# Gates matrix of a product-key expert layer made once for all 128 first parts, a quarter kept in SBUF and the rest read back from DRAM in blocks

## The chip, the cores and the metric

The kernel runs on one core of one Trainium2 chip. The metric is the device time of one execution in microseconds (us). TensorE (PE) multiplies matrices and loads its weights in a row of its own (PEld), VectorE (DVE) and ScalarE (ACT) do the elementwise work, GpSimd (POOL) issues the gathers of rows and some subtractions, and SyncE (SP) issues all other transfers, in order, on one queue. Sixteen DMA engines carry the transfers of both queues.

## The reference

Two layers, each with token mixers (pooling, Mamba-2, gated DeltaNet, Fourier) and then a retrieval of experts (PEER). The change is in the second part, of which this is the core:

```python
def one_block(hb):                       # hb: [tokens, 1024]
    q = (hb @ wq).reshape(t, 8, 2, 128)
    s = jnp.einsum('thsd,hskd->thsk', q, sub_keys)
    v1, i1 = lax.top_k(s[:, :, 0], 16)
    v2, i2 = lax.top_k(s[:, :, 1], 16)
    cand = v1[..., :, None] + v2[..., None, :]          # 16 x 16 sums a head
    cid = i1[..., :, None] * 128 + i2[..., None, :]     # number of the expert
    best, pos = lax.top_k(cand.reshape(t, 8, 256), 16)
    eid = jnp.take_along_axis(cid.reshape(t, 8, 256), pos, axis=-1)
    gate = jax.nn.softmax(best, axis=-1)
    act = gelu(jnp.einsum('td,thkd->thk', hb, u_tab[eid]))
    return jnp.einsum('thk,thkd->td', gate * act, v_tab[eid])
```

There are 16384 experts, 128 first parts by 128 second parts, 512 tokens, 8 heads, and 16 experts a head: 128 slots a token.

## The kernel before

Of the four token tiles of 128 in a layer, three (ND = 3, 384 tokens) take the dense way: the activations of all experts are computed and multiplied by a matrix of gates that is zero for the experts a token did not choose. The fourth tile gathers the rows of its own experts (`gather`): 128 gathers of 512 KB from the table u and 128 from v, each followed by one DVE instruction of 1024 columns.

The dense way has two loops over c, the 128 first parts.

- `dense_u`: for each c it loads 512 KB of u (`du`), splits it into a high and a low part (`dh` on ACT, `dl` on DVE or POOL), multiplies both with the hidden state (24 matmuls of 384 columns), applies Gelu on ACT (`da`) and writes 192 KB to DRAM (`acts`). 56 of its 128 steps run as filler beside the search for the top experts. The other 72 run in a loop of `run`, with one step of `gates_slice` after every third (GSK = 3) and four gathers to every three steps (GU) as side work.
- `dense_v`: for each c it reads `acts` back (`a`), loads 512 KB of v (`dv`), splits v, multiplies `a` with the gates of this first part, splits that, and adds up 18 matmuls of 512 columns into six PSUM banks that are held over the whole loop. The tiles of the split stand in the memory of the hidden states and so are called `hx` in the profile. `a` and `dv` have three buffers each, the split tiles two and four. Side work again is four gathers to every three steps (GV).

The gates matrix W is [128 second parts, first parts, tokens]. For each token it is a product of two one-hot matrices over its 128 slots: B (slot by second part) and A (slot by first part, times the gate, in two float16 parts). `gates_slice` makes it for 32 first parts and 16 tokens at a time: two matmuls of 32 columns a token, 32 in a group, all into one PSUM bank, and one ACT instruction from there into W. A slice is 24 such groups, and a layer has four slices. Slice 0 is made in the loop of `dense_u`; it also makes B on DVE, casts it to float8 on ACT and writes it to DRAM (`hot`). Slices 1 to 3 are made along `dense_v`, three groups to every four c, each after reading its B back from `hot`. W is double buffered, and at every 32nd c the loop goes on to the slice that was just finished.

The order on each engine is fixed when the program is built, by priorities and by the class `Order`, which puts side work behind the main step before it.

Of the kernel before, what the change touches and what calls it, by code (L numbers as in the profile page):

```python
# [10 lines left out]
F32 = mybir.dt.float32  # L11
# [21 lines left out]
# the 16 best sums of two descending lists of 16 lie where (a + 1) * (b + 1) <= 16  # L33
# [33 lines left out]
B8 = 2  # L67
# [9 lines left out]
# input projection, in units of 256 columns  # L77
U_XBC, U_QKV, U_Z, U_GZ, U_POOL, U_FOUR, U_GATE = 0, 4, 10, 12, 14, 16, 18
# per-partition vectors
# [4 lines left out]
# the gates' scale in float16: two parts hold them to float32's last bit, down to 2 ** -17  # L84
# [5 lines left out]
class Stored:  # L90
    """A state kept in DRAM."""
# [5 lines left out]
class Filler:  # L97
    """Work that is put between the steps of a chain, a piece at a time."""
# [5 lines left out]
class Section:  # L104
    """A part of the program: the last instruction of each engine in it."""
# [6 lines left out]
class Order:  # L112
    """Steps of a loop and side work between them, in order: both wait for the side work of some steps before."""
# [20 lines left out]
class Engine:  # L134
    """An engine whose instructions join the open sections."""
# [20 lines left out]
class Region:  # L156
    """Memory that is cut by hand into tiles of several kinds."""
# [21 lines left out]
class K:  # L179
    """The program: tiles, constants and the parts of a layer."""  # L180
# [41 lines left out]
    def add(self, gen, pre="x", after=None):  # L222
        """To the end of the queue, or as far to the front as can be behind another."""
        f = Filler(gen, pre)
        at = len(self.fillers)
        if after is not None:
            at = int(at > 0 and self.fillers[0].begun)
            if after in self.fillers:
                at = self.fillers.index(after) + 1
        self.fillers.insert(at, f)  # L230
        return f

    def step(self, f):
        """A piece of f; whether there was one."""
# [16 lines left out]
    def tick(self, n):  # L251
        """The next n rows, behind what there is of the main work."""
# [26 lines left out]
    def fill(self, n=1):  # L279
        """The next n pieces."""  # L280
        while n and self.fillers:
            n -= self.step(self.fillers[0])

    def finish(self):
        """The rest of the work that has begun."""
        if self.fillers:
            f = self.fillers[0]
            while self.step(f):
                pass
# [6 lines left out]
    @contextmanager  # L296
    def phase(self, name, side="left", **bufs):
        """Tiles of a part of the program; their memory is used again by the next part."""
# [10 lines left out]
    def keep(self, shape, tag, bufs=1, dt=F32):  # L309
        """A tile that lives across phases."""  # L310
# [3 lines left out]
    def t(self, shape, tag, bufs=1, dt=F32, area=None):  # L314
        """A tile of its own kind in the current phase."""
# [7 lines left out]
    def sharing(self):  # L323
        """The phases within share the tiles of weights and loads of the current one."""
# [5 lines left out]
    def lane(self, pre):  # L330
        """Tiles of their own for a part that runs beside another in the same phase."""
# [4 lines left out]
    def s2(self, shape=(128, 512), dt=F32):  # L336
        """A tile of up to 2 KB a partition."""
# [5 lines left out]
    def sm(self, shape, tag, bufs, dt=F32):  # L343
        """A tile of up to 1 KB a partition: among the others of that size if the phase has them."""
        return self.s2(shape, dt) if self.pre + "s1" in self.bufs else self.t(shape, tag, bufs, dt)

    def s4(self, shape=(128, 1024), dt=F32):
        """A tile of up to 4 KB a partition."""
# [4 lines left out]
    def x4(self):  # L353
        """A tile of 4 KB a partition, loaded."""
# [4 lines left out]
    def ld(self, shape=(128, 512)):  # L359
        """A tile of up to 2 KB a partition, loaded."""  # L360
        return self.t(shape, "ld", self.bufs.get("ld", LDB))

    def hx(self, dt=F32R):
        """The memory of the hidden states: [128, 2, 8, 512]."""
# [3 lines left out]
    def cut(self, **bufs):  # L368
        """A part of the program whose tiles are cut from the memory of the hidden states."""
# [11 lines left out]
    def pa(self):  # L381
        """A bank that is held for long."""
# [7 lines left out]
    def consts(self):  # L390
# [9 lines left out]
        # 0 .. 15; where the pairs of the k-th best first part begin, and how far they are apart  # L400
# [6 lines left out]
        for l in range(L):  # L407
# [4 lines left out]
            # A = exp(a_log)  # L412
# [4 lines left out]
    def rsqrt(self, out, x, scale, eps):  # L417
        """out = (x * scale + eps) ** -0.5 for a few columns."""
# [5 lines left out]
    def split(self, hi, lo, x):  # L424
        """x = hi + lo exactly, both of float32r."""
# [13 lines left out]
    def load_w(self, src, held=False):  # L439
        """Weights [128, 2, 256], split; held for longer than the others."""  # L440
# [19 lines left out]
    def mod_steps(self, l, groups, fm):  # L460
        """FM columns [128, 48, 2] of (shift1, 1 + scale1, gate1, shift2, 1 + scale2, gate2)."""
# [27 lines left out]
    def bcast_row(self, fm, g, s, scale):  # L489
        """[128, 1024]: part g of the modulation of stream s along the free axis, in every partition."""  # L490
# [25 lines left out]
    def norm_mod(self, x, fm, g, s, hT, keep=None):  # L516
        """hT hi/lo: eight tiles [128, T] each; the first columns whole into keep [128, 8, ..]."""
# [7 lines left out]
    def modulated(self, i, y, fm, g, s, hT):  # L525
        """The hidden state of a normed token tile into hT."""
# [42 lines left out]
    def residual(self, x, out, mix, l, fm, g, s, scale, gi):  # L569
        """LayerNorm(alpha x + gate * mix) into out; mix(i, q) gives half a token tile, which is used up."""  # L570
# [20 lines left out]
    def residual_steps(self, x, out, mix, rows, normed=None):  # L591
        """A token tile of the residual, in four steps; its layer norm too if normed is a list."""
# [40 lines left out]
    def proj_fm(self, src, unit, h, T, fn):  # L633
        """fn(j, psum) for the feature tiles of one unit."""
# [11 lines left out]
    def proj_tm(self, src, unit, h, NT, fn):  # L646
        """fn(i, psum [128, 256]) for the token tiles of one unit."""
# [11 lines left out]
    def conv_silu(self, l, tile_i, ps, T, bias):  # L659
        """Twice silu of the convolution, FM."""  # L660
# [18 lines left out]
    def scan_scalars(self, l, h, NT):  # L679
        """dt [128, NT, 24], la [128, NT, 24] (log decays), beta [128, NT, 8], and exp of their sums  # L680
        EX [128, 3, NT, 24]: up to and with the token, past it, over the tile."""
# [21 lines left out]
        # softplus(z) = max(z, 0) + log1p(exp(-|z|))  # L703
# [3 lines left out]
        # log1p(e) = 2 atanh(e / (2 + e))  # L707
# [15 lines left out]
        # beta = 1 / (1 + exp(-b))  # L723
# [13 lines left out]
    def decay(self, la, out_mask, in_mask):  # L737
        """E [128 a, 4, 128 b] = exp of the sum over k of out_mask[k, a] la[k, h] in_mask[k, b]."""
# [14 lines left out]
    def ssd_local(self, l, c, sx, sb, sc, dt, la, EX, full):  # L753
        """Local part of a tile, both directions: y [128, 512] and the states the tile adds."""
# [53 lines left out]
    def ssd_step(self, c, d, sc, S, st, EX, y):  # L808
        """y += C S exp(decay); S <- S * exp(total) + st"""
# [3 lines left out]
        if y is not None:  # L813
# [7 lines left out]
            # sc is twice silu  # L821
# [8 lines left out]
    def gdn_norm(self, qk, NT):  # L830
        """qk: 8 FM tiles of twice silu (q, k); the normalised ones into (k, q) tiles."""
# [10 lines left out]
        # both hold twice the value: the norm's guard counts four times  # L842
# [12 lines left out]
    def gdn_tokens(self, c, kf, vf):  # L855
        """k and v of a tile by token,."""
# [13 lines left out]
    def gdn_A(self, c, d, la, beta, kf):  # L870
        """A below the diagonal: by rows for the forward direction, transposed for the other."""
# [16 lines left out]
    def gdn_blocks(self, G):  # L888
        """In DRAM: G matrices by rows, and the diagonal blocks of their inverses and those transposed among zeros."""
# [10 lines left out]
    def gdn_inv(self, G, blocks, F):  # L900
        """Inverses of the 32 x 32 diagonal blocks of I + A, one in a partition."""
# [27 lines left out]
    def gdn_whole(self, i, d, blocks):  # L929
        """The inverse of matrix i of direction d: what the products take as their stationary operand, the inverse  # L930
        itself or its transpose."""
# [4 lines left out]
        # 32 -> 64  # L936
# [14 lines left out]
        # 64 -> 128  # L951
# [15 lines left out]
    def gdn_uw(self, c, d, X, kt, vt, kf, qf, la, beta, EX, full):  # L967
        """u [128, 4, 128], wT [128 k, 4, 128], kd [128, 4, 128], at [128 j, 4, 128 i]."""
# [45 lines left out]
    def gdn_step(self, c, d, S, u, w, kd, at, qf, EX, o):  # L1014
        """One tile of the scan; S None stands for zeros. Returns the next state, adds to o[c]."""
# [1006 lines left out]
```

## Time and profile before

| | before |
|---|---|
| median of 3 runs | 6059.81 us (6032.5 to 6069.9) |
| profiled execution, first to last instruction | 6038.3 us |
| PE busy | 5335.8 us, 88% |
| DVE busy | 4268.9 us, 71% |
| ACT busy | 2029.4 us, 34% |
| POOL busy | 1759.7 us, 29% |
| moved by DMA | 1385.55 MB, mean 229 GB/s |

The page gives no other time of the profiled execution than its span of 6038.3 us; it lies inside the range of the three runs, 21.5 us under their median. A busy share is an average over stages: the experts' loops are two stretches of the span, in layer 0 from about 2450 to 3520 us and in layer 1 from about 4970 to 6010 us, and only the rows of those stretches say what bounds them. In a profile line of an instruction, L144 is the helper that issues every instruction, so the groups are told apart by the names of the tiles.

### The profile page before, as it was taken

To read this page: it belongs to the slowest core of one execution; us is meant where nothing else is said; L and a number is where in the kernel's file an instruction comes from. 1 tells how busy PE (TensorE), PEld (TensorE's weight loads), DVE (VectorE), ACT (ScalarE), POOL (GpSimd) and SP (SyncE) were. 2 spreads that over 40 slices of the span, in tenths; PEclk is the share of its full clock that TensorE was granted. 3 is DMA by queue.
4 is the path that set the end of the run, shared out by engine and by line. 5 is a ranking of instruction groups with operands and counts; after the bars stand their busy time and mean duration, and the time that the engine had idled before them with its cause. 6 is when DMAs were issued, how large, how long until landed. Compare 5 with 4: busy or idle time off the path is not lost. (4 is left out here: it accounts for less than half of the span.)

```text
span 6038.3 us, 86377 instructions
## 1 busy us (share of the span) xinstructions
PE 5335.8 (88%) x31510; PEld 4517.3 (75%) x31510; DVE 4268.9 (71%) x8383; ACT 2029.4 (34%) x3375; POOL 1759.7 (29%) x1338
## 2 busy tenths in 40 slices
PE   8988978986566877899999979999898889999998
PEld 3887855733565777898888768776787889988886
DVE  4756287787888888777777786566565747677778
ACT  2444412320123232344333354332234334433333
POOL 0001544224544766432222300000004433322222
PEclk9999988997688988999999999999998999999999
DMA  6556479788887766998887854333444349988887
GB/s 214 179 162 202 134 243 310 245 273 308 265 300 249 239 198 232 321 309 297 275 285 269 312 181 141 120 119 109 129 142 133 117 166 315 310 283 275 277 284 254
DMA packets 597274, 1385.55 MB, mean 229 GB/s; under 512 B 100080, under 2 KB 186736, under 8 KB 596848
## 3 DMA queue, kind: packets, MB, share of 16 engines
q1 hardware_dynamic: 449392, 843.10, 41.5%
q0 software_dynamic: 147456, 536.94, 26.6%
q8 instruction: 247, 4.05, 0.3%
q14 instruction: 179, 1.47, 0.1%
HBM read 1244.52 MB, written 135.27 MB: 229 GB/s over the span
## 5 line engine op out<-in xcount | busy, mean ns | idle before, releaser
L144 POOL DMA_INDIRECT gat<-in_u,gidx x512 | 609.1, 1190 | 1129.6 <-DVE gat L144 1053.9
L144 POOL DMA_INDIRECT gat<-in_v,gidx x512 | 624.4, 1219 | 1067.7 <-DVE gacc L144 929.4
L144 DVE SCALAR_TENSOR_TENSOR gacc<-gat,gact,gacc 128x1024 f32<-128x1024 f32 x508 | 691.1, 1360 | 96.8 <-DMA gat<-in_v,gidx 93.0
L144 PE MATMUL ps<-hx 128*128 128x512 f32 x3072 | 751.6, 393 | 0.0
L144 DVE SCALAR_TENSOR_TENSOR gat<-gat,hb 128x1024 f32<-128x1024 f32 x512 | 618.5, 1220 | 100.7 <-DMA gat<-in_u,gidx 100.1
L144 PEld LDWEIGHTS ps<-hx 128*128 128x128 f32 x3072 | 584.7, 190 | 125.8
L144 PE MATMUL ps<-hx,dh 128*128 128x384 f32 x2304 | 595.9, 340 | 6.2 <-ACT dh L144 6.2
L144 PE MATMUL ps<-s,s 128*128 128x128 f32 (+3 forms) x2752 | 416.3, 308 | 157.1 <-issue 88.9
L144 PEld LDWEIGHTS ps<-s,s 128*128 128x128 f32 (+1 forms) x2752 | 372.1, 212 | 227.9 <-issue 124.5
L144 PE MATMUL pa<-hx,dh 128*128 128x384 f32 x1792 | 518.9, 360 | 6.2 <-ACT da L144 4.4
L144 ACT CAST dh<-du 128x1024 fp32r<-128x1024 f32 x256 | 268.9, 1051 | 714.6 <-issue 279.8
L144 DVE TENSOR_TENSOR hx<-dv,hx 128x1024 fp32r<-128x1024 f32 x256 | 313.4, 1224 | 255.8 <-ACT hx L144 245.6
L144 ACT CAST hx<-dv 128x1024 fp32r<-128x1024 f32 x256 | 269.1, 1051 | 567.1 <-PE ps L144 447.5
L144 PE MATMUL pa<-hx 128*128 128x512 f32 x1536 | 417.7, 406 | 31.7 <-ACT hx L144 30.8
L144 PEld LDWEIGHTS <-B 128*128 128x128 fp8e4 x6144 | 405.1, 155 | 50.2 <-issue 44.9
L144 PE MATMUL ps<-A,B 128*128 128x32 f16 x6144 | 434.5, 246 | 5.0 <-ACT B L144 5.0
L144 PEld LDWEIGHTS ps<-hx,dh 128*128 128x128 f32 x2304 | 417.9, 189 | 8.4 <-ACT dh L144 8.4
L144 PE MATMUL ps<-hx,whi 128*128 128x512 f32 x1152 | 388.5, 405 | 19.2 <-ACT whi L144 19.2
L144 PE MATMUL ps<-hx,dl 128*128 128x384 f32 x1152 | 389.2, 338 | 13.4 <-DVE dl L144 13.4
L144 ACT CAST xwhi<-xwraw 128x512 fp32r<-128x512 f32 x352 | 218.5, 621 | 530.8 <-PE pa L144 401.3
L144 PE MATMUL pa<-hx,xwhi 128*128 128x512 f32 x1152 | 380.5, 404 | 10.0 <-DVE ld L144 5.1
L144 PE MATMUL pa<-hx,dl 128*128 128x384 f32 x896 | 326.0, 364 | 64.3 <-POOL dl L144 49.2
(282 smaller groups left out, 10573.2 us busy)
## 6 DMA issues: line engine op xcount, KB each, us to landing
du<-in_ut SPq DMA_DIRECT2D x256, 512.0 KB
dv<-in_v SPq DMA_DIRECT2D x256, 512.0 KB
xwraw<-in_w_in SPq DMA_DIRECT2D x272, 256.0 KB
acts<-da SPq DMA_DIRECT2D x256, 192.0 KB
a<-acts SPq DMA_DIRECT2D x256, 192.0 KB
wraw<-in_w_in SPq DMA_DIRECT2D x176, 256.0 KB
xwraw<-in_w_mod SPq DMA_DIRECT2D x160, 256.0 KB
B<-hot SPq DMA_DIRECT2D x144, 256.0 KB
```

The source lines that it names most:

```text
L144: r = f(*a, **kw)
```

## The change

All 128 first parts are made in one pass of 24 groups (`gates_all`), in the loop of `dense_u`, one group in place of each group of slice 0. A group still has 32 matmuls, now of 128 columns, over four PSUM banks, and eight ACT instructions that take the results out. B stays in float16 in SBUF and is neither cast nor written. The gates of the first 32 first parts (WR) stay in SBUF as W, now laid out by group of 16 tokens; those of the other 96 go into a tile `wst` and from there to DRAM (`rest`), 768 KB a group. `dense_v` makes no gates; it reads `rest` back in six blocks of 16 first parts (WK), 3 MB each, into two buffers `wk`, at c = 8, 24, 48, 64, 80 and 96. The memory of what made the gates is given up before `dense_v`. Comments were dropped as well.

```diff
-B8 = 2
+WR = 32
+WK = 16
...
-    def gates_slice(self, sl, it, gp, W, hot):
-        def products(t0, B, A):
-            ps = self.p((128, 16, 32))
-            for k in range(16):
-                for q in range(2):
-                    nc.tensor.matmul(ps[:, k, :], B[:, :, k], A[:, q, :, k], start=q == 0, stop=q == 1)
-            nc.scalar.activation(W[:, :, t0:t0 + 16], ps.rearrange("p t i -> p i t"), AF.Copy, scale=1 / GATE)
+    def gates_all(self, it, gp, W, rest):
+        def products(g, B, A):
+            st = self.t((128, 128 - WR, 16), "wst", 2)
+            for n in range(4):
+                ps = self.p((128, 4, 128))
+                for k in range(4):
+                    for q in range(2):
+                        nc.tensor.matmul(ps[:, k, :], B[:, :, 4 * n + k], A[:, q, :, 4 * n + k], start=q == 0,
+                                         stop=q == 1)
+                r = ps.rearrange("p t i -> p i t")
+                for out, part in ((W[:, g], r[:, :WR]), (st, r[:, WR:])):
+                    nc.scalar.activation(out[:, :, 4 * n:4 * n + 4], part, AF.Copy, scale=1 / GATE)
+            nc.sync.dma_start(rest[g], st.rearrange("p i t -> p (i t)"))
...
-            B = self.t((128, 128, 16), "B8", B8, F8)
-            if sl == 0:
-                b = self.t((128, 128, 16), "B", 1, F16)
-                nc.vector.tensor_tensor(b, it[1][:, None, t].to_broadcast([128, 128, 16]), self.iota, op=OP.is_equal)
-                nc.scalar.copy(B, b, saturate=False)
-                nc.sync.dma_start(hot[t0 // 16], B)
-            else:
-                nc.sync.dma_start(B, hot[t0 // 16])
-            e = self.t((128, 32, 16), "A", 2, F16)
...
+        for g in range(ND * 8):
+            t = slice(16 * g, 16 * g + 16)
+            shape = [128, 128, 16]
+            B = self.t(shape, "B", 2, F16)
+            nc.vector.tensor_tensor(B, it[1][:, None, t].to_broadcast(shape), self.iota, op=OP.is_equal)
+            e = self.t(shape, "A", 1, F16)
+            nc.vector.tensor_tensor(e, it[0][:, None, t].to_broadcast(shape), self.iota, op=OP.is_equal)
+            A = self.t((128, 2, 128, 16), "A2", 2, F16)
             for q in range(2):
-                nc.vector.tensor_tensor(A[:, q], e, gp[:, q, None, t].to_broadcast([128, 32, 16]), op=OP.mult)
+                nc.vector.tensor_tensor(A[:, q], e, gp[:, q, None, t].to_broadcast(shape), op=OP.mult)
...
-    def dense_v(self, l, acts, it, gp, acc, W, area, other, made, hot):
+    def dense_v(self, l, acts, acc, W, rest, area, other, made):
...
-            if c % 32 == 0:
-                self.run_all(gen)
-                W, Wn = (W, None) if c == 0 else (Wn, None)
-                if c == 96:
-                    made()
-                if c < 96:
-                    sl = c // 32 + 1
-                    Wn = self.t((128, 32, T), "W", 1, F32, None if sl % 2 == 0 else area)
-                    gen = self.gates_slice(sl, it, gp, Wn, hot)
-            elif c % 4:
+            if len(blocks) < (128 - WR) // WK and c == (WK // 2 + len(blocks) * WK if len(blocks) < 2 else
+                                                        WR + (len(blocks) - 1) * WK):
+                m = len(blocks)
                 with go.side():
-                    next(gen, None)
+                    blocks[m] = self.t((128, ND * 8, WK * 16), "wk", 2, F32, area)
+                    nc.sync.dma_start(blocks[m], rest[:, :, m * WK * 16:(m + 1) * WK * 16].rearrange("g p x -> p g x"))
+            if c == 96:
+                made()
...
-            nc.vector.tensor_mul(a, a, W[:, c % 32, :])
+            if c < WR:
+                w = W[:, :, c]
+            else:
+                m = (c - WR) // WK
+                w = blocks[m][:, :, (c - WR) % WK * 16:(c - WR) % WK * 16 + 16]
+            a3 = a.rearrange("p (g t) -> p g t", t=16)
+            nc.vector.tensor_mul(a3, a3, w)
...
-            dd.enter_context(self.phase("wp"))
+            dd.enter_context(self.phase("wr"))
+            W = self.t((128, ND * 8, WR, 16), "W")
+            rest = self.d([ND * 8, 128, (128 - WR) * 16], "rest")
+            wp = ExitStack()
+            wp.enter_context(self.phase("wp"))
...
-            W = self.t((128, 32, ND * 128), "W")
-            hot = [self.d([128, 128, 16], "hot", 24, F8) for _ in range(24)]
-            gs = self.gates_slice(0, it, gp, W, hot)
+            gs = self.gates_all(it, gp, W, rest)
...
             self.run_all(gs)
+            wp.close()
```

## Rows read from the trace of the kernel before

**Rows 1.** Stretches in layer 1: loop of `dense_u`, `dense_v` with gates, twice without.

```profile
core 0: us, PE busy (x) PEld busy (x) DVE busy (x) ACT busy (x) POOL busy (x), PEclk, DMA share, GB/s
5100.00:5200.00 100.00, 100.00 (x703) 98.89 (x702) 69.03 (x101) 44.67 (x55) 31.83 (x27) 1.00 0.92 311
5350.00:5500.00 150.00, 150.00 (x1109) 127.40 (x1108) 114.25 (x190) 51.31 (x71) 34.53 (x35) 1.00 0.84 288
5880.00:5920.00 40.00, 40.00 (x178) 33.12 (x177) 33.45 (x41) 14.10 (x18) 15.17 (x12) 1.00 0.93 323
5920.00:5960.00 40.00, 40.00 (x178) 33.12 (x177) 36.49 (x44) 15.27 (x20) 16.82 (x14) 1.00 0.97 346
```

**Rows 2.** The same view in layer 0: `dense_v` with gates, then without.

```profile
2900.00:3000.00 100.00, 100.00 (x737) 84.69 (x736) 75.09 (x122) 33.39 (x47) 23.86 (x24) 1.00 0.83 289
...
3400.00:3450.00 50.00, 41.89 (x166) 33.41 (x165) 47.23 (x66) 18.40 (x27) 19.63 (x15) 0.90 0.85 307
```

**Rows 3.** Chain that ended last: start, length, what; `dense_v` of layer 1.

```profile
5615.72 2.72 PE ps L144 x12
...
5638.56 2.74 PE ps L144 x12
...
5884.91 2.72 PE ps L144 x12
5888.99 2.72 PE ps L144 x12
```

**Rows 4.** Timeline around c = 32: the change of slices.

```profile
5500.13 2.26 PE L144 MATMUL ps<-A,B 128*128 128x32 f16 x32
...
5503.06 1.49 DVE L144 TENSOR_TENSOR a<-a,W 128x384 f32<-128x384 f32 x3 [0.42 <-ACT W L144]
...
5504.21 2.01 PE L144 MATMUL pa<-hx 128*128 128x512 f32 x4 [1.82 <-ACT hx L144]
...
5508.20 0.63 PE L144 MATMUL pa<-hx 128*128 128x512 f32 x2
```

**Rows 5.** Groups by form: count, busy us, mean ns of one, idle before.

```profile
L144 PE MATMUL ps<-A,B 128*128 128x32 f16 x6144 | 434.5, 246 | 5.0 <-ACT B L144 5.0
...
L144 DVE TENSOR_TENSOR A<-A,gp 128x512 f16<-128x512 f16 x384 | 146.4, 421 | 4.1
...
L144 ACT ACTIVATE W<-ps 128x512 f32<-128x512 f32 x192 | 115.1, 600 | 193.5 <-PE ps L144 191.9 <-issue 1.7
...
L144 ACT CAST B<-B 128x2048 fp8e4<-128x2048 f16 x48 | 90.8, 1891 | 11.5 <-DVE B L144 11.5
...
L144 DVE TENSOR_TENSOR B<-it,iota 128x2048 f16<-128x2048 f16 x48 | 58.6, 1221 | 0.0
...
L144 ACT ACTIVATE da<-ps 128x384 f32<-128x384 f32 x144 | 69.7, 485 | 15.2 <-PE ps L144 7.4 <-issue 5.8 <-DMA acts<-da 2.0
```

**Rows 6.** Timeline of PE in the loop of `dense_u`, around one group of gates.

```profile
5227.68 0.51 PE L144 MATMUL ps<-hx,dh 128*128 128x384 f32 x2
5228.20 2.26 PE L144 MATMUL ps<-A,B 128*128 128x32 f16 x32
5230.27 0.60 PE L144 MATMUL ps<-hx,dh 128*128 128x384 f32 x2
```

**Rows 7.** Timeline of PE, weights of 256 columns, early in layer 0.

```profile
91.31 0.40 PE L144 MATMUL ps<-hT,whi 128*128 128x256 f32 x2
...
91.67 0.40 PE L144 MATMUL ps<-hT,whi 128*128 128x256 f32 x2
```

**Rows 8.** Timeline of DVE in the same loop: a splitting waits, later between gates.

```profile
5235.68 1.23 DVE L144 TENSOR_TENSOR dl<-du,dh 128x1024 fp32r<-128x1024 f32 x1 [2.60 <-ACT dh L144]
...
5244.70 1.21 DVE L144 TENSOR_TENSOR dl<-du,dh 128x1024 fp32r<-128x1024 f32 x1
5245.84 0.75 DVE L144 TENSOR_TENSOR A<-A,gp 128x512 f16<-128x512 f16 x2
```

**Rows 9.** DMA from 3398 to 3420 us, in `dense_v` of layer 0.

```profile
DMA packets 2940, 8.56 MB, mean 389 GB/s; under 512 B 332, under 2 KB 1169, under 8 KB 2938
```

More of the change, by code (lines that the diff above doesn't have):

```diff
@@ L1618, in dense_in @@
         nc.vector.tensor_sub(gp[:, 1, t], g, gp[:, 0, t])
-    def gates_slice(self, sl, it, gp, W, hot):
+    def gates_all(self, it, gp, W, rest):
         nc = self.nc
-        def products(t0, B, A):
-            ps = self.p((128, 16, 32))
-            for k in range(16):
-                for q in range(2):
-                    nc.tensor.matmul(ps[:, k, :], B[:, :, k], A[:, q, :, k], start=q == 0, stop=q == 1)
-            nc.scalar.activation(W[:, :, t0:t0 + 16], ps.rearrange("p t i -> p i t"), AF.Copy, scale=1 / GATE)
-        made = None
-        for t0 in range(0, ND * 128, 16):
-            t = slice(t0, t0 + 16)
-            B = self.t((128, 128, 16), "B8", B8, F8)
-            if sl == 0:
-                b = self.t((128, 128, 16), "B", 1, F16)
-                nc.vector.tensor_tensor(b, it[1][:, None, t].to_broadcast([128, 128, 16]), self.iota, op=OP.is_equal)
-                nc.scalar.copy(B, b, saturate=False)
-                nc.sync.dma_start(hot[t0 // 16], B)
-            else:
-                nc.sync.dma_start(B, hot[t0 // 16])
-            e = self.t((128, 32, 16), "A", 2, F16)
-            nc.vector.tensor_tensor(e, it[0][:, None, t].to_broadcast([128, 32, 16]),
-                                    self.iota[:, 32 * sl:32 * sl + 32, :], op=OP.is_equal)
-            A = self.t((128, 2, 32, 16), "A2", 2, F16)
@@ L1647, in gates_slice @@
             if made:
                 products(*made)
-            made = t0, B, A
+            made = g, B, A
             yield
@@ L1670, in dense_u @@
             yield
-    def dense_v(self, l, acts, it, gp, acc, W, area, other, made, hot):
+    def dense_v(self, l, acts, acc, W, rest, area, other, made):
         nc = self.nc
         T = ND * 128
-        gen = iter(())
         cut = Region(self.hx(F32).rearrange("p a b c -> p (a b c)"))
         go = Order(self, VO)
+        blocks = {}
         for c in range(128):
-            if c % 32 == 0:
-                self.run_all(gen)
-                W, Wn = (W, None) if c == 0 else (Wn, None)
-                if c == 96:
-                    made()
-                if c < 96:
-                    sl = c // 32 + 1
-                    Wn = self.t((128, 32, T), "W", 1, F32, None if sl % 2 == 0 else area)
-                    gen = self.gates_slice(sl, it, gp, Wn, hot)
-            elif c % 4:
+            if len(blocks) < (128 - WR) // WK and c == (WK // 2 + len(blocks) * WK if len(blocks) < 2 else
+                                                        WR + (len(blocks) - 1) * WK):
+                m = len(blocks)
                 with go.side():
-                    next(gen, None)
+                    blocks[m] = self.t((128, ND * 8, WK * 16), "wk", 2, F32, area)
+                    nc.sync.dma_start(blocks[m], rest[:, :, m * WK * 16:(m + 1) * WK * 16].rearrange("g p x -> p g x"))
+            if c == 96:
+                made()
             for _ in range(GV[c % len(GV)]):
@@ L1884, in run @@
                 acc = [[self.pa() if 2 * b + q < PA else self.p() for q in range(2)] for b in range(ND)]
-                self.dense_v(l, acts, it, gp, acc, W, vv, gen, made, hot)
+                self.dense_v(l, acts, acc, W, rest, vv, gen, made)
                 self.run_all(gen)
```

## The prediction

> **What bounds the kernel now.** I read the stretches of the two loops first, because the page's 88% for PE is a mean over stages. In layer 1 PE is busy for all of 100 us in the loop of `dense_u` and all of 150 us in `dense_v`, at a granted clock of 1.00, which is its level of 2.4 GHz, while DVE stands at 69% and 76% and ACT at 45% and 34% [rows 1]. Layer 0 is the same while gates are made; only in its last quarter of `dense_v`, where DVE also does a residual, is DVE the fuller engine, 47 of 50 us [rows 2]. The chain of waits then says what PE does there: it runs from matmul to matmul with nothing between. Four steps with three groups of gates begin 22.84 us apart; a step without gates takes 4.08 us [rows 3]. So in `dense_v` time is matmul time, and what is taken off PE there comes off the end, as long as DVE and the DMA engines can keep a pace of 4.08 us. The two stretches without gates show that they can, narrowly: PE stays full with DVE at 84 and 91% and the DMA engines at 323 and 346 GB/s, a share of 0.93 and 0.97 [rows 1]. That is the view to keep in mind: PE is the limit, and two others stand right behind it.
>
> **Gates out of `dense_v`.** (22.84 - 4 x 4.08) / 3 = 2.17 us a group. A layer has 6144 / 2 / 32 = 96 groups [rows 5], 24 of them in `dense_u`; the other 72 lie on PE's chain: 72 x 2.17 = 156 us a layer, 313 us in both.
>
> **The changes of slice.** At c = 32 the last group ends in a wait: its eviction into W, the product `a` x W on DVE, the splitting, and only then matmuls. PE sits for 1.82 us, and its next ten matmuls of 512 columns take 5508.20 - 5504.21 = 3.99 us where a step's pace gives 10 x 4.08 / 18 = 2.27 [rows 4]. That is 3.5 us, at three places in each layer: 21 us, which go, since the block for c = 32 is asked for at c = 8. What is late next at these places is the next matmul, at 4.08 us a step.
>
> **Wider gates in `dense_u`.** The group stays at 32 matmuls, of 128 columns and not 32. The group of 32 columns takes 5230.27 - 5228.20 = 2.07 us, 65 ns a pair of weight load and matmul [rows 6]. No row shows float16 at 128 columns. Three rows bound it: 4.08 / 18 = 227 ns at 512 columns, 0.52 / 3 = 173 ns at 384 (two of one tile, one of another between the starts [rows 6]), 0.36 / 3 = 120 ns at 256 [rows 7]. The line through them falls by 53 ns for 128 columns and gives 67 ns at 128, hardly more than the 65 ns at which the pair stands already. From below I take no loss, 65 ns; from above all 96 added columns at 53 / 128 ns, 105 ns. I take 70 ns: 48 groups x 32 x 5 ns = 8 us; bounds 0 and 61 us. The Trainium skill, "TensorE: Matmul & The Clock Gate", section "Back-to-back issue gap", speaks against so small a cost: it gives about 81 ns a matmul for a sustained stream of pairs at 128 columns. By that the term would be 48 x 32 x 16 ns = 25 us (an estimate from the page). The same passage gives 131 ns at 512 columns where this trace has 227, so I keep to the rows.
>
> **DVE and ACT in `dense_u`.** DVE makes B as before and now A and its two parts at 2048 columns, where it had 512: three times 1.22 - 0.42 = 0.8 us, 2.4 us a group [rows 5]. A period of three steps and a group is 72 x 0.174 + 2.07 = 14.6 us, and DVE has 31% of it free, 4.5 us [rows 1]. One splitting waits 2.60 us for ACT, and another is slipped in among the instructions of a group, so the pieces of a group don't all stand ahead of a splitting [rows 8]. I cost this at nothing; without that cover it is 48 x 2.4 = 115 us. ACT loses the cast (1.89 us) and one eviction (0.60 us) and gains eight evictions of 128 or 384 columns, each at most the 0.485 us that Gelu takes for 384 [rows 5]: at most 1.4 us more a group, in an engine that is 55% idle [rows 1]. Nothing. After the last group there are four banks to evict and not one before c = 0 can be multiplied: 2 us a layer, 4 us in all, between 0 and 6.
>
> **Transfers in `dense_u`.** A group writes 0.79 MB to `rest` where it wrote 0.26 MB to `hot`: 0.52 MB in 14.6 us, 36 GB/s on top of 311 [rows 1], so 347. In this mix no row shows more than a share of 0.92 at 311; in `dense_v` of layer 0, over 22 us of backlog, 389 GB/s were moved [rows 9]. If 389 holds here, the cost is 0; if 311 is all, it is 36 / 311 of 24 x 14.6 = 350 us, 41 us a layer. I take 10 us a layer, 20 us, near the free end, because 346 GB/s were carried at a full PE [rows 1]; bounds 0 and 82. SP issues one write a group as before, which now waits for eight evictions and not for a cast; queued behind it are the next loads of `du`, which have three buffers of lead.
>
> **Blocks in `dense_v`.** A layer reads 6 x 3.15 = 18.9 MB of gates, as much as the 72 reads of `hot` brought; but they now run at 4.08 us a step and not 5.7. The steps alone need 323 to 346 GB/s [rows 1]; a block in every 16 steps (65 us) adds 48, so 371 to 394, against 389 seen [rows 9]. At 389 nearly all is hidden: 0. At 346 with nothing to spare a block costs 3.15 MB / 346 GB/s = 9.1 us, and if PE then starts anew as at c = 32 another 1.7 us [rows 4]: 65 us a layer. Behind a block on SP stand the loads of `a` and `dv`; three buffers and two split tiles are some 16 us of lead, more than a block needs, but it must be won back before the next one. I take the middle of 0 and 9.1, 5 us a block: 60 us in both layers, bounds 0 and 130.
>
> **Sum.** 313 + 21 - 8 - 4 - 20 - 60 = 242 us. From the profiled span of 6038 us that leaves 5796; the median of the runs is 22 us over that span, and the same difference from 6060 gives **5818 us**.
>
> **The rivals.** (1) PE alone remains: the wider group is free and 389 GB/s are held for the whole loop. Then 313 + 21 - 8 - 4 = 322 us go: 5738. For it speaks PE's full row at 346 GB/s; against it that 389 was seen for 22 us only, with DVE and not PE the full engine around it [rows 2]. The Trainium skill, "DMA: Bandwidth & Descriptors", section "Specifications", gives a core about 358 GB/s of HBM traffic. By that this rival can't be, and the 424 us of the 104 steps with blocks on the way would stretch by (382 / 358 - 1) x 424 = 28 us a layer (an estimate from the page). The 389 GB/s pass that figure, if for 22 us alone; without them I would give this rival half its chance. (2) The DMA engines become the bound at about 346 GB/s: blocks at their full 130 us, `dense_u` at half of its dear end, 41 us in both layers. Then 313 + 21 - 8 - 4 - 130 - 41 = 151 us: 5909. For it speaks the share of 0.97; against it the 389. (3) Slower: PE in `dense_u` waits at every group, because SP holds the loads of `du` behind a write to `rest`, or DVE's four instructions of 1.22 us come ahead of a splitting. 242 us over 48 groups is 5.0 us: from a wait of that length at each group the change loses. Half a period lost, 7.3 us, would cost 350 us and give 6168. Against it: the splitting slipped in among a group [rows 8], and three buffers of `du`. (4) PE's time does not go, since DVE takes the place: at 4.08 us a step DVE is at 84 to 91% [rows 1]. If it also waits for gathers that come late, PE waits for it: 1.2 us a step over 96 steps are 230 us in both layers, and 12 us of gain stay: 6048, no change. Against it: the gathers came in time at 346 GB/s [rows 1].
>
> **How the numbers follow.** Forecast 0.62, rival 1 0.12, rival 2 0.14, rival 3 0.07, rival 4 0.05. The range of 8 in 10 goes from rival 1's 5738, less the 8 us of the wider group, 5730, to rival 2's 5909 with the wider group at its upper bound, 53 us more: 5960. A measurement of this kernel can tell about 1% from no change, 61 us, so faster begins under 5999: forecast, rivals 1 and 2 give 0.88, less 0.03 for all terms at their dear ends at once (334 - 61 - 6 - 82 - 130 = 55 us of gain: 6005). Same: 0.07. Slower: 0.08, rival 3 and a little of rival 4.
>
> **What would show it.** Right: the chain in `dense_v` runs at 4.08 us a step from c = 1 on, `dense_v` is some 135 us a layer shorter, PE's gates appear only in `dense_u` at about 2.2 us a group, and DMA there and in `dense_v` stands above 340 GB/s. A wait of `hx` or `a` for DMA of some 5 us after each block is the term of the blocks; none would be rival 1. Wrong: gaps of PE in `dense_u` ahead of `dl` or `du` (rival 3), DVE near 100% with PE waiting in `dense_v` (rival 4), or matmuls of 128 columns at 100 ns.

## The result and the profile after

The changed kernel takes 6213.68 us (median of 4 runs, 6211.86 to 6226.05) beside 6052.93 for the kernel before on the same chip: ratio 1.0283, 95% interval [1.0261, 1.0304]. It is slower. The profiled execution spans 6210.5 us, against 6038.3. So the sign was wrong, and the question is where the 242 us of gain that were forecast went.

First the page's engine line, to set beside 88% for PE before.

```profile
PE 5393.9 (87%) x26902; PEld 4458.5 (72%) x26902; DVE 4243.6 (68%) x7951; ACT 1961.0 (32%) x3519; POOL 1833.3 (30%) x1338
```

PE is as busy as before, over a longer span, with 4608 fewer matmuls of gates: others must have become dearer. To place that, the spans of three tiles are enough. The view of tile `pa` (the products of `dense_v`) first in the trace of before, then in that of after: name and count, shortest/median/longest ns of one, first and last start in us, a row for each layer (layer 0 of before is its first).

```profile
L144 PE MATMUL pa<-hx x768: 387/389/796, 2815.2 to 3527.1; 128*128 128x512 f32 x192
L144 PE MATMUL pa<-hx x768: 387/389/796, 5314.5 to 6006.9; 128*128 128x512 f32 x192
```

```profile
L145 PE MATMUL pa<-hx x768: 388/389/797, 2976.0 to 3594.8; 128*128 128x512 f32 x192
L145 PE MATMUL pa<-hx x768: 388/389/796, 5573.5 to 6179.1; 128*128 128x512 f32 x192
```

`dense_v` goes from 711.9 and 692.4 us to 618.8 and 605.6: 180 us gained, where the prediction had some 270. The loop of `dense_u` is taken from its first gate matmul to the first load of `dv`. In layer 1 the views of tiles `B` and `dv` have these two starts (before, then after):

```profile
L144 PE MATMUL ps<-A,B x2304: 233/246/266, 4977.3 to 5689.1; 128*128 128x32 f16 x192
L144 SPq DMA_DIRECT2D dv<-in_v x128: 327/382/2122, 5303.5 to 5992.5; - x128
```

```profile
L145 PE MATMUL ps<-A,B x768: 411/423/452, 5063.4 to 5565.2; 128*128 128x128 f16 x192
L145 SPq DMA_DIRECT2D dv<-in_v x128: 332/333/10727, 5567.3 to 6165.6; - x128
```

The loop goes from 341.2 us (2464.0 to 2805.2, layer 0) and 326.2 to 508.6 (2461.2 to 2969.7) and 503.9: 345 us lost, where the prediction had 28. Around them +7 us is left: the way from layer 0's `dense_v` to layer 1's first gates is 18 us longer, the starts of `dense_v` are 8.5 us shorter, 3 us go ahead of layer 0's first gates, and the tail is the same. -180 + 345 + 7 = 172 us, the difference of the spans. So there are two things to explain: 345 us in `dense_u`, and 90 us that `dense_v` failed to give.

**`dense_u`.** PE's timeline in the loop of `dense_u` of layer 1, to be set beside [rows 6]:

```profile
5306.61 7.88 PE L145 MATMUL ps<-A,B 128*128 128x128 f16 x32
5314.13 1.00 PE L145 MATMUL ps<-hx,dh 128*128 128x384 f32 x2
...
5317.17 0.60 PE L145 MATMUL ps<-hx,dh 128*128 128x384 f32 x2
5317.79 0.51 PE L145 MATMUL ps<-hx,dh 128*128 128x384 f32 x2
```

From the group's start to the next tile's: 7.52 us for 32 matmuls, 235 ns each, against 2.07 us before. The next two matmuls of 384 columns are recorded with 1.00 us where they take 0.60 and 0.51 a little later. The windows of the same stretch say why: the three stretches inside the group and the one behind it have a granted clock that falls.

```profile
5250.00:5350.00 100.00, 100.00 (x475) 88.18 (x475) 55.36 (x65) 30.75 (x60) 23.05 (x17) 0.83 0.72 232
5299.00:5306.60 7.60, 7.60 (x45) 7.46 (x43) 5.44 (x7) 2.14 (x4) 1.37 (x2) 1.00 0.64 190
5308.00:5310.00 2.00, 2.00 (x10) 1.20 (x8) 2.00 (x3) 0.74 (x3) 1.85 (x1) 1.00 0.74 145
5310.00:5312.00 2.00, 2.00 (x10) 1.27 (x9) 2.00 (x3) 0.67 (x2) 0.13 (x1) 0.63 1.06 324
5312.00:5314.10 2.10, 2.10 (x11) 1.27 (x10) 1.86 (x3) 0.66 (x2) 0.00 (x0) 0.50 0.62 226
5315.50:5317.20 1.70, 1.70 (x7) 1.70 (x7) 0.00 (x0) 0.00 (x0) 0.00 (x0) 0.50 0.65 72
5319.00:5327.00 8.00, 8.00 (x47) 8.00 (x47) 4.19 (x5) 2.88 (x4) 0.94 (x1) 1.00 0.77 253
```

In the first row PE is busy for 100 of 100 us, as it was in [rows 1], with 475 matmuls where it had 703. (A stretch also counts a matmul that only reaches into it, so the short ones count one or two too many.) Inside the group the pace is the same at either level: in the timeline matmuls start 0.24 us apart at a granted clock of 1.00 (5308.56, 5308.80, 5309.04) and 0.24 us apart at 0.50 (5312.64, 5312.88, 5313.12). What the group waits for does not go with TensorE's clock. But the clock falls from 2.4 to 1.2 GHz during it, and the nine matmuls that follow pay for that before it is back: they take 3.04 us (5314.13 to 5317.17) where nine at 174 ns would take 1.57. A period grew by (508.6 - 341.2) / 24 = 6.97 us in layer 0 and by 7.40 in layer 1: 7.52 - 2.07 = 5.45 for the group, and 1.5 behind it at the half clock.

DVE is less busy than before, and PE waits only at the entrance of the loop: 3.63 us in layer 0, where it waited 12.1 before (most of why layer 0's periods grew by less), and 10.35 us in layer 1 ahead of the first group, which is a part of the 18 us above (the same timeline, earlier; in brackets the idle time ahead and who ended it):

```profile
5057.88 0.69 PE L145 MATMUL ps<-hx,dl 128*128 128x384 f32 x1 [10.35 <-DVE dl L145]
```

**`dense_v`.** Its chain of waits, start, length, what, shows steps of matmuls with loads between them. A layer has six blocks; in layer 1 the chain has such a wait behind five of them. Behind the first, asked for at 5601.12 us, the chain runs elsewhere, but there too PE is busy for only 28.96 of the 39 us from 5601 to 5640.

```profile
5693.54 12.18 DMA dv<-in_v
...
5806.65 13.43 DMA dv<-in_v
...
5869.99 2.72 PE ps L145 x12
...
5875.13 23.58 DMA dv<-in_v
...
5903.24 3.40 PE ps L145 x12
...
5954.32 23.87 DMA dv<-in_v
...
6031.40 23.80 DMA a<-acts
```

SP's timeline at the third of these places:

```profile
5873.55 0.43 SPq L145 DMA_DIRECT2D wk<-rest  x1
5875.13 10.21 SPq L145 DMA_DIRECT2D dv<-in_v  x1
5885.43 0.38 SPq L145 DMA_DIRECT2D a<-acts  x1
```

The block is asked for, SP then sits 10.21 us in the issue of the next load, and the load of `a` behind that goes out only after it. DVE gets its `a` at 5899.25 and had waited 9.39 us for it:

```profile
5899.25 0.56 DVE L145 TENSOR_TENSOR a<-a,wk 128x384 f32<-128x384 f32 x1 [9.39 <-DMA a<-acts]
```

The DMA view from 5866 to 5900 us (of each queue: packets, MB, share of the 16 engines) has the gathers, q0, taking 45% of the engines' time beside the 57% of SP's queue, q1, in which the block lies:

```profile
DMA packets 6080, 12.43 MB, mean 366 GB/s; under 512 B 351, under 2 KB 4054, under 8 KB 6078
...
q1 hardware_dynamic: 4491, 6.63, 56.5%
q0 software_dynamic: 1587, 5.77, 45.2%
```

So 6.63 MB in 34 us pass q1, 195 GB/s, and a block of 3.15 MB alone needs 16 us at that rate, with loads around it more.

### The profile page after: what moved, and what is told of

Same layout as the page of the kernel before. It is cut to its first block, busy times and chain, and to the rows that moved or that the text cites. A ratio compares the mean times of both kernels' runs of the same rounds, so it can differ in the third digit from the quotient of the medians.

```text
span 6210.5 us, 76829 instructions
## 1 busy us (share of the span) xinstructions
PE 5393.9 (87%) x26902; PEld 4458.5 (72%) x26902; DVE 4243.6 (68%) x7951; ACT 1961.0 (32%) x3519; POOL 1833.3 (30%) x1338
## 4 chain that ended last, share of the span: by engine, by line
PE 46%; issue 17%; DMA 12%; DVE 11%; POOL 7%; ACT 2%; SPq 0%; POOLq 0%; ACTq 0%; DVEq 0%
PE ps L145 30%; PE pa L145 16%; POOL gat L145 6%; DMA gat<-in_v,gidx 3%; DMA dv<-in_v 3%; DVE s L145 2%; DVE oh L145 2%; DVE gacc L145 1%; DMA a<-acts 1%; DVE gat L145 1%; DMA gat<-in_u,gidx 1%; DMA xwraw<-in_w_mod 1%; DMA wraw<-in_w_out 1%; DVE hx L145 1%; ACT s L145 1%
## 5 line engine op out<-in xcount | busy, mean ns | idle before, releaser
L145 POOL DMA_INDIRECT gat<-in_u,gidx x512 | 652.6, 1275 | 1391.0 <-DVE gat L145 1311.7
L145 POOL DMA_INDIRECT gat<-in_v,gidx x512 | 653.4, 1276 | 892.8 <-DVE gacc L145 769.4
L145 PE MATMUL ps<-hx,dh 128*128 128x384 f32 x2304 | 664.2, 373 | 1.4 <-ACT dh L145 1.4
L145 DVE TENSOR_TENSOR dl<-du,dh 128x1024 fp32r<-128x1024 f32 x160 | 195.3, 1223 | 470.9 <-ACT dh L145 470.7
L145 PEld LDWEIGHTS ps<-hx,dh 128*128 128x128 f32 x2304 | 476.9, 214 | 7.1 <-ACT dh L145 3.0
L145 PEld LDWEIGHTS pa<-hx 128*128 128x128 f32 x1536 | 296.1, 196 | 227.5 <-ACT hx L145 146.7
L145 PE MATMUL ps<-hx,dl 128*128 128x384 f32 x1152 | 422.6, 367 | 20.4 <-DVE dl L145 20.4
L145 PE MATMUL ps<-hx,whi 128*128 128x512 f32 x1152 | 385.7, 402 | 13.9 <-ACT whi L145 13.9
L145 PE MATMUL ps<-A,B 128*128 128x128 f16 x1536 | 377.5, 423 | 0.0
```

The lines of the kernel that those rows point to most:

```text
L145: r = f(*a, **kw)
```

## The experiments

Two theories were put to the test, each with its rivals. **M**: TensorE reads a moving operand whose columns lie far apart slowly; a column of `A` lies 32 bytes behind the last one, and there are four times as many now. Its rivals: it is the weights `B`, with 32-byte columns too (**W**), or the width as such (**C**). **Q**: what `dense_v` lost is the blocks, each one lump in SP's queue ahead of the loads of `dv` and `a`; its rival is that the bytes are too many for the DMA engines (**D**). "Pieces" below is a block read in 12 parts of 256 KB, one each step.

**e1: `A` laid out token by token in SBUF, so that its 128 columns lie 2 bytes apart.** `B` and all else stay.

```diff
-A = self.t((128, 2, 128, 16), "A2", 2, F16)
+A = self.t((128, 2, 16, 128), "A2", 2, F16)
-nc.vector.tensor_tensor(A[:, q], ...)
+nc.vector.tensor_tensor(A[:, q].rearrange("p t i -> p i t"), ...)
...
-nc.tensor.matmul(ps[:, k, :], B[:, :, 4 * n + k], A[:, q, :, 4 * n + k], ...)
+nc.tensor.matmul(ps[:, k, :], B[:, :, 4 * n + k], A[:, q, 4 * n + k], ...)
```

> The gates' moving operand A is laid out token by token, so that each matmul reads 128 columns that lie side by side and not 32 bytes apart; the weights B stay 32 bytes apart. Theory M (the columns of the moving operand, 32 bytes apart, come in at about 1.9 ns each and set 235 ns a matmul): a group falls from 7.5 us to about 2.2 us, the granted clock stays at 1.00 in the loop of dense_u, that loop is some 165 us a layer shorter, total about 5885 us. Theory W (the weights, 32 bytes apart, set it): group and total unchanged, 6214. Theory C (128 columns of float16 in four banks with their evictions cost that in any layout): unchanged, 6214.

Measured: 6718.68 us, and in PE's timeline (first fence) and the groups by form (second: mean ns behind the comma):

```profile
2617.48 2.22 PE L145 MATMUL ps<-A,B 128*128 128x128 f16 x32
2619.51 0.59 PE L145 MATMUL ps<-hx,dh 128*128 128x384 f32 x2
```

```profile
L145 DVE TENSOR_TENSOR A<-A,gp 128x2048 f16<-128x2048 f16 x96 | 887.6, 9433 | 0.1
```

The group falls from 7.52 to 2.03 us, 63 ns a matmul, and the matmul behind it is back at 0.59: M. The total of about 5885 us that M expected did not come: the price has moved to DVE, which now writes elements 256 bytes apart and takes 9.43 us for 2048 of them where 1.22 was the price [rows 5], and the kernel as a whole is slower still.

**e2: the same for `B` alone**, `A` as in the changed kernel (`B` of shape (128, 16, 128), read as `B[:, 4 * n + k]`).

> Only the weights B are laid out token by token; A stays 32 bytes apart. Theory M: group 7.5 us as before, total 6214. Theory W: group about 2.2 us, total about 5885. Theory C: unchanged.

Measured: 6297.66 us; the group takes 7.22 us (2612.49 to 2619.71). Of the 5.45 us 0.3 are gone at most: W is out. Width as such is out with e1. The total is 84 us above what M expected; here it is `B` that DVE writes 256 bytes apart, in 9.36 us.

**e8: the kernel before, its 32 columns of `A` side by side** (the same three lines there). It asks whether the dear columns were in the old kernel too, unseen.

> The kernel before with the columns of A side by side, 32 of them. Theory L (before, the weights' pace of 63 ns and 32 columns of 1.84 ns, 59 ns, lay so near each other that the row couldn't tell them apart): its group stays at 2.0 to 2.07 us. If the 65 ns were the columns alone: 1.5 us or less. DVE writes 512 columns with a stride twice a group, about 2.3 us each, so the total is 6050 to 6200.

Measured: 6384.94 us, above the 6050 to 6200 expected; DVE's writing, 2.63 us where it was 0.42, is again what grew. PE's timeline and the groups by form:

```profile
2611.21 2.11 PE L144 MATMUL ps<-A,B 128*128 128x32 f16 x32
2613.16 0.60 PE L144 MATMUL ps<-hx,dh 128*128 128x384 f32 x2
```

```profile
L144 PE MATMUL ps<-A,B 128*128 128x32 f16 x6144 | 411.9, 212 | 57.8 <-DVE A L144 52.7 <-ACT B L144 5.0
...
L144 DVE TENSOR_TENSOR A<-A,gp 128x512 f16<-128x512 f16 x384 | 929.5, 2628 | 1.3
```

The group takes 1.95 us with columns side by side and 2.07 with columns 32 bytes apart: no difference that mattered. From the 235 ns of the changed kernel, a column 32 bytes apart costs 235 / 128 = 1.84 ns, so 32 of them 59 ns by this estimate: hidden under the 65 ns at which the pair of weight load and matmul stood. By it the two costs nearly coincided, and the old trace looked as if columns were free. It did hold a hint: the mean duration of one of those matmuls, 246 ns [rows 5], is 34 ns longer than the 212 of e8.

**How far apart may they lie? e5, e6, e9, e11.** `A` in tiles of TG tokens, the tokens of a tile side by side, so that columns lie 2 x TG bytes apart; blocks in pieces.

```diff
-A = self.t((128, 2, 128, 16), "A2", 2, F16)
+A = self.t((128, 2, 16 // TG, 128, TG), "A2", 2, F16)
-nc.tensor.matmul(ps[:, k, :], B[:, :, 4 * n + k], A[:, q, :, 4 * n + k], ...)
+nc.tensor.matmul(ps[:, k, :], B[:, :, 4 * n + k], A[:, q, (4 * n + k) // TG, :, (4 * n + k) % TG], ...)
```

e5 (TG 4) and e6 (TG 8) make it in 16 / TG instructions of DVE each; e9 (TG 2) and e11 (TG 4) in one, with an access pattern of four dimensions.

```diff
+row = lambda x: x.rearrange("p (h t) -> p h t", t=TG)[:, :, None, :].to_broadcast([128, 16 // TG, 128, TG])
...
-nc.vector.tensor_tensor(A[:, q], e, gp[:, q, None, t].to_broadcast(shape), op=OP.mult)
+nc.vector.tensor_tensor(A[:, q], e, row(gp[:, q, t]), op=OP.mult)
```

The factor `e`, which DVE makes ahead of that, takes the same order of elements, with a small tile of numbers for it.

e5:

> A is made for 4 tokens at a time, in tiles [first part, 4 tokens], so that DVE still writes side by side and a matmul reads its columns 8 bytes apart; the blocks are read in pieces as in the run before. If the cost of a column follows its distance (1.84 ns at 32 bytes, so 0.46 at 8): the weights' 63 ns set the pace, a group takes about 2.05 us, the granted clock stays at 1.00 in dense_u, DVE needs 0.9 us a group more, total 5740 to 5800. If any distance costs the full 1.84 ns: group 7.5 us, total about 6080 as with the pieces alone.

e6:

> The same for 8 tokens at a time: columns 16 bytes apart. Cost in proportion to the distance: 0.92 ns a column, 118 ns a matmul, group 3.8 us, total about 80 us above the run with 8 bytes. Full cost at any distance: group 7.5 us, total about 6080. No cost below 32 bytes: group 2.05 us.

e9:

> Columns of A 4 bytes apart (two tokens side by side), blocks read in pieces; DVE makes each of its four tiles of a group in one instruction of 2048 elements. If the cost of a column goes on falling with its distance below 8 bytes (0.93 ns there, so about 0.47 at 4): weights' pace, group 2.05 to 2.2 us, total 5837 - 48 x 1.7 = 5750 to 5765, if DVE still takes 1.2 us an instruction. If it takes 2.3 us, as with the broadcast, DVE is full in dense_u: 5850 to 5900.

e11:

> Columns 8 bytes apart as in the first run of that distance, but each DVE tile in one instruction of 2048 elements: group on PE 3.82 us again, DVE 0.5 to 0.9 us a group less if the pattern with one more dimension costs nothing; total 5825 to 5840, since PE is the limit in dense_u and not DVE.

Measured, with the group's time from PE's timeline (in brackets its start and that of the next tile):

| columns apart | group, us | ns a matmul | kernel, us |
|---|---|---|---|
| 2 bytes (e1, whole blocks) | 2.03 | 63 | 6718.68 (DVE) |
| 4 bytes (e9) | 2.08 | 65 | 5749.54 |
| 8 bytes (e5) | 3.82 (2567.76 to 2571.58) | 119 | 5837.38 |
| 8 bytes, one DVE instruction (e11) | 3.82 (2564.17 to 2567.99) | 119 | 5838.52 |
| 16 bytes (e6) | 7.32 (2618.26 to 2625.58) | 229 | 6056.62 |
| 32 bytes (changed kernel, whole blocks) | 7.52 | 235 | 6213.68 |

e5 came out between its two expectations: 8 bytes are neither free nor at the full cost. e6 came out at the second of its three: 16 bytes cost nearly all that 32 do, not half. The cost is one of steps: free to 4 bytes, 0.93 ns a column at 8, 1.8 from 16 on. The Trainium skill, "SBUF — State Buffer", section "Door 1: The DMA port swizzle", says that SBUF is read in lines of 16 bytes and that two or more accesses to a line are needed for full bandwidth. That the cost stops growing at 16 bytes agrees with it (one column to a line, 229 and 235 ns); at 8 bytes there are two to a line and the group still took 3.82 us, not 2.08, and there the measurement decides. e11 takes DVE one instruction of 2048 elements where e5 takes four of 512, and comes to the same time: at 8 bytes PE and not DVE sets it.

e9 in PE's timeline, and three of its windows, one in the loop of `dense_u` and two in `dense_v` (columns as in [rows 1]):

```profile
2604.22 2.27 PE L145 MATMUL ps<-A,B 128*128 128x128 f16 x32
2606.30 0.59 PE L145 MATMUL ps<-hx,dh 128*128 128x384 f32 x2
```

```profile
2600.00:2700.00 100.00, 100.00 (x712) 98.91 (x711) 86.58 (x102) 45.22 (x98) 43.77 (x27) 1.00 0.97 342
...
5400.00:5500.00 100.00, 100.00 (x442) 82.52 (x441) 91.63 (x106) 37.68 (x49) 41.73 (x34) 1.00 1.04 394
5500.00:5600.00 100.00, 99.96 (x441) 82.26 (x440) 91.13 (x107) 37.91 (x50) 42.80 (x33) 1.00 1.04 396
```

With the group back at 2.08 us the granted clock is 1.00 in `dense_u`, there are 712 matmuls in 100 us where there were 475, and DVE's instruction is still at 1.22 us. 5749.54 us is 0.9515 [0.9499, 0.9531] of the kernel before (6038.05 beside it): this version beats both kernels. Against the changed one it differs in the order of `A`'s elements and in the blocks' pieces, no more; against e3 (below), which has the pieces too, in the order alone, and its two loops of `dense_u` are 334 us shorter than e3's (348.3 and 330.7 us against 509.0 and 504.1).

**e7: the other way to please both engines.** DVE writes `A` token by token, 128 elements in a row, and reads the token's value with a stride of zero; pieces.

```diff
-nc.vector.tensor_tensor(A[:, q], e, gp[:, q, None, t].to_broadcast(shape), op=OP.mult)
+nc.vector.tensor_tensor(A[:, q], e, gp[:, q, t, None].to_broadcast([128, 16, 128]), op=OP.mult)
...
```

> A is written token by token with all 128 columns side by side; DVE now reads the gate and the number of a token as one value for 128 columns and writes side by side. Group on PE 2.03 us. If what made DVE take 9.3 us in the run with A alone was the writing 256 bytes apart: three instructions of 1.2 to 2.2 us, total 5760 to 5860. If it is the order of the elements itself: 9 us again, total above 6500.

Measured: 5898.47 us. The group takes 2.02 us (2603.24 to 2605.26), but DVE's instruction 2.28 us and not 1.22:

```profile
L145 DVE TENSOR_TENSOR A<-A,gp 128x2048 f16<-128x2048 f16 x96 | 215.5, 2285 | 0.0
```

Better than 8 bytes apart on PE, dearer on DVE, and the total misses the 5760 to 5860 expected and is behind e9 by 149 us.

**e4: no blocks read at all.** It leaves out the reads and takes the gates of c - 32, c - 64 or c - 96 in their place (`w = W[:, :, c % WR]`), so its output is another one.

> The blocks aren't read: every first part is multiplied with the gates of the first 32, so the sum is that of other gates. If the blocks are all that holds dense_v above 4.08 us a step (theories Q and D): dense_v 75 to 80 us a layer shorter, total about 6060, PE full from the first step to the last in layer 1. If DVE or the gathers hold it: less than half of that, total above 6140.

Measured: 6042.07 us, 172 less than the changed kernel. In layer 1, the tile `pa` and a window of `dense_v`:

```profile
L145 PE MATMUL pa<-hx x768: 388/389/795, 5481.0 to 6002.5; 128*128 128x512 f32 x192
```

```profile
5600.00:5700.00 100.00, 100.00 (x443) 82.82 (x442) 91.53 (x108) 38.38 (x50) 41.95 (x33) 1.00 0.96 347
```

521.5 us are 128 steps of 4.07, and layer 0 takes 531.9 (2966.0 to 3497.9). So the two gains did come in full: 711.9 - 531.9 + 692.4 - 521.5 = 351 us for the gates and the changes of slice. And with the blocks, in the changed kernel, 86.9 + 84.1 = 171 us of it go again, 14 us for each of the twelve.

**e3: the changed kernel with its blocks in pieces.**

```diff
-nc.sync.dma_start(blocks[m], rest[:, :, m * WK * 16:(m + 1) * WK * 16].rearrange("g p x -> p g x"))
+m, g = todo.pop(0)      # one in each step
+nc.sync.dma_start(blocks[m][:, g:g + 2], rest[g:g + 2, :, m * WK * 16:(m + 1) * WK * 16].rearrange("g p x -> p g x"))
```

> Each block of 3.1 MB is read in 12 pieces of 256 KB, one for each first part, instead of with one transfer. Theory Q (the loads of a and dv stand behind 3.1 MB in SP's queue, longer than their lead): PE's waits of 8 to 24 us after each block go, dense_v 60 to 75 us a layer shorter, total 6065 to 6095. Theory D (the DMA engines can't carry 18.9 MB a layer more at this pace): the waits only spread out, total 6170 to 6214.

Measured: 6080.42 us, 133 less than the changed kernel with the same bytes on the way; `dense_v` takes 554.8 us (2972.4 to 3527.2) and 530.2 (5510.6 to 6040.8), so that the blocks still cost 32 us of 171. The bytes as such have no more than that; the rest is how they are asked for.

**e10 and e12: on top of e9, whole blocks again; in e12 asked for from ACT's queue** (`nc.scalar.dma_start` in place of `nc.sync.dma_start`). They part two halves of Q: the order in one queue, and the lump itself.

> The same layout of A, but each block read whole, with one transfer as in the change: the change with the one fault of the strided columns mended. If the cost of the blocks doesn't depend on dense_u: 133 us above the run with pieces, 5885 to 5900. That would be the prediction's sum with the blocks at 22 us each and not 5.

> Columns of A 4 bytes apart, each block read whole as in the change, but issued by ACT, on a queue of its own. Theory Q (what costs is that a and dv stand behind 3.1 MB in SP's queue): the loads go past the block, total near the run with pieces, 5750 to 5790. Theory S (3.1 MB at once take the DMA engines from a, dv and the gathers, in whatever queue): total near the run with whole blocks, 5870 to 5910.

Measured: e10 5901.99 us (0.9778 [0.9763, 0.9792]), 152 above e9; e12 5841.28 us (0.967 [0.964, 0.9701]), 61 below e10 and 91 above e9. Neither half has it all. In e10's chain the loads of `dv` behind a block wait as in the changed kernel:

```profile
5559.59 23.32 DMA dv<-in_v
```

In e12's chain they wait 5 us and those of `a` 5 to 11; once it is the block that comes last:

```profile
5661.03 22.70 DMA wk<-rest
```

The view of tile `wk` in e12 has that for all twelve:

```profile
DMA to landing us min/median/max: 20.1/23.2/24.6
```

So two fifths of the 152 us come back when the block leaves SP's queue. The loads behind it show why: SP's longest issue of a load of `dv` falls from 13.9 us (e10) to 1.7, and the longest of these loads from issue to landing from 25.1 us to 12.7, as in e9. The block itself lands no sooner, after 23.2 us (median) beside 24.6 in e10. That the other three fifths are 3.15 MB at once crowding the engines beside the gathers is what is left over, and was not shown by itself.

## Why the prediction was wrong

**What bounds the kernel**: right. PE is busy for 99 to 100% of both loops in e4 and 96 to 99% in e9, and time taken off it came off the end.

**Gates out of `dense_v` and changes of slice**: right, 313 + 21 = 334 us forecast, 351 measured (e4). No run shows where the 17 us more come from.

**Wider gates in `dense_u`**: here the sign was lost. Forecast 8 us with bounds of 0 and 61; the matmuls of the group alone cost 48 x 5.45 = 262 us, and the half clock behind them 48 x 1.5 = 72, in sum 334, which is also what the loops of e3 and e9 differ by. The step took 70 ns for a matmul, from lines through rows of 512, 384 and 256 columns [rows 6, 7], and bound 105 ns by adding columns at that slope. Those rows are of operands whose columns lie side by side; the gates' columns lie 32 bytes apart, and the row nearest in kind, the group of 32 such columns [rows 6], could not show it, because (by the estimate under e8) 59 ns of columns lay under 65 ns of pairs. The bound should have been worked out from that row: if all of its 65 ns were columns, 128 of them take 4 x 65 = 260 ns, 299 us for the 48 groups. For the width alone the 70 ns were good: e9 has 65. The prediction's list of what would make it wrong had "matmuls of 128 columns at 100 ns"; they came, at 235. The second part, the clock, had no place in the sum.

**DVE and ACT**: right as to cover: in the changed kernel and in e9 neither holds PE once the loop runs. At its entrance PE waits for `dl`, 10.35 us in layer 1 of the changed kernel, 12.78 and 10.21 in the two layers of e9: the form of rival 3, once in a layer and not at every group.

**Transfers in `dense_u`**: forecast 20 us with a bound of 82. In e9, where PE sets the pace again, the loop takes 348.3 and 330.7 us, 7 and 4.5 above before; no more than that is left for this term, and 3 us of it are the longer waits at layer 0's entrance. The loop moves 342 GB/s at a full PE.

**Blocks**: forecast 60 us, at most 130; measured 171. The bound was the DMA engines' rate, 9.1 us a block, and a new start. What the runs show in its place is the lump: 3.15 MB in front of loads in one queue, which shares the engines with gathers and has some 200 of the 366 GB/s, so that a load behind it lands after 23.6 us and not within the 16 of lead. "More than a block needs" was the sentence that failed. Rival 2, the rate, is not it: in pieces the same bytes cost 32 us. Of what the lump costs, the order in SP's queue is two fifths (e12); the cause of the rest stays open.

The sum with measured terms is 351 - 262 - 72 - 12 - 171 = -166, and with the 7 us around the loops -173, beside -172 between the spans.

**Rivals**: none of them was the case. Rival 3 had the sign, and its threshold of 5.0 us a group was passed with 6.97 and 7.40; but PE was held by its own matmuls and not by a wait. Rival 1 had PE alone at 5738, and e9, with the group free and 394 and 396 GB/s carried for 100 us each, comes to 5749.54. The 358 GB/s of the Trainium skill's page, "DMA: Bandwidth & Descriptors", against which the prediction weighed that rival, did not bind here; the section "Bandwidth" of that page has it for two cores that share a memory stack and stream together, and here one core ran.

## What to carry to other kernels

When a tile gets wider, work out what its columns cost from the old row of the same tile as if nothing else were in it: of two costs that run beside one another the smaller is hidden at the old size, and rows of operands with another layout say nothing about it. A layout has two users: choose it so that the writer and the reader are both at full pace (here 4 bytes for TensorE, one instruction for DVE), and try it in the group's rows before the whole. A large read that has time to spare goes out in pieces among the small ones that have none.

## What the runs showed of the hardware

- A matmul of float16 with 128 moving columns takes 63 ns with columns 2 bytes apart, 65 at 4, 119 at 8, 229 at 16 and 235 at 32; with the columns at 32, weights laid side by side changed 235 to 226 (e2).
- The pace of such a group, with columns 32 bytes apart, does not go with the granted clock: the matmuls start 0.24 us apart at 1.00 and at 0.50. PE was busy without a gap before and in the group (5306.61 to 5314.13 us), and the granted clock went from 1.00 to 0.50 within it; it was 0.50 to 5317.2 us and 1.00 again from 5319 us, with matmuls of 384 columns. Over 2600 to 2700 us, in the same loop, it was 1.00 with groups of 3.82 us (e5) and 0.83 with groups of 7.32 (e6).
- DVE's product of 2048 float16 takes 1.22 us where it writes in a row, 9.43 us where it writes 256 bytes apart (e1), and 2.28 us where the innermost stride of an input is zero (e7); of 512 elements 0.42 us in a row and 2.63 us at 64 bytes apart (e8).
- One core moved 394 and 396 GB/s over two stretches of 100 us, with PE full (e9).
